# A hybrid decoder layer on one Trainium2 core: gate columns in column groups, the small delta-net inverse by blocks of four and doubling, product groups farther apart

## The chip, the core and the metric

The kernel runs on one NeuronCore of one Trainium2 chip. The metric is the device time of one execution in microseconds; three runs of the kernel before gave a median of 2695.42 us (2695.19 to 2695.53). Engine names are those of the profile: PE multiplies matrices (PEld loads its weights), DVE, ACT and POOL work elementwise, SP only issues DMAs.

## What is computed

One layer of a decoder on 512 new positions of one sequence and on 8 short sequences of 8 positions that carry states, 576 columns in all, everything in fp32. The part that matters here, cut from the reference:

```python
h = _rmsnorm(x, norm_mix_g)                       # x: 576 x 2048
proj = jnp.einsum('bld,de->ble', h, w_in)         # q, k, v, z of 8 delta-net heads, 4 mLSTM heads, and 24 gate columns
beta = jax.nn.sigmoid(dn_b)                       # gate columns: one row per head
g = -jnp.exp(dn_A_log) * jax.nn.softplus(dn_a + dn_dt_bias)
logf = jax.nn.log_sigmoid(ml_f + ml_f_bias)
...
G = jnp.cumsum(g, axis=-1)                        # delta net, by chunks
lower = jnp.where(strict, jnp.einsum('nbhik,nbhjk->nbhij', kb, k) * decay, 0.0)
a_mat = lower + jnp.eye(c)
u = solve(a_mat, v * beta[..., None])             # unit lower triangular
w = solve(a_mat, kb * jnp.exp(G)[..., None])
...
x = x + einsum(mix, w_out); x = x + ConvFFN(rmsnorm(x)); final rmsnorm
```

The triangular solves are done with the explicit inverse of each 128x128 unit triangle.

## The kernel before

Activations lie transposed: 16 tiles of 128 features by 576 columns (`KT` = 16, `NT` = 576, `HALF` = 288). A dense product of fp32 operands is made of three products of their high and low parts (line 198, `three`): per k-step of 128 features 2 halves x 3 products = 6 matmuls of 128x288, and a dense tile of 128 output features (`dense`) has 16 k-steps, 96 matmuls. Its weights come as two units of 128x1024 (512 KB), which `load_unit` brings (line 129, two raw buffers) and splits: ACT casts the high part (`wh`, line 120), DVE subtracts for the low part (`wl`, line 121), two buffers each.

PE's order is the order in which the program is written (`manual_schedule`); the other engines' order comes from a scheduler with priorities. Between the k-steps of the dense tiles a job list is ticked (`tick`, once a k-step): each job is a generator, and `yield n` means that its next piece is written n k-steps later. So the dense tiles fill PE, and the pieces of the heads are strewn between them; a piece whose operands are late stops PE, since nothing behind it overtakes.

- `startup` (line 332) loads `par` (all small parameters, POOL queue), the 16 tiles of x (line 351) and the first weight units, forms the scaled high and low parts `ah`, `al` (lines 356 and 357), and then squares x on ACT (line 363) and adds the squares on DVE and POOL in turn (lines 365 and 366).
- `gates` loads the constants `con` and the convolution state `dnst` on the POOL queue, makes small tables, and multiplies the padded tile of gate columns as the first dense tile of all, 96 matmuls into two PSUM banks.
- `gate_rows` waits 14 k-steps, sums the squares over the features with two fp32 matmuls of ones (line 256, 128x288 each), makes the reciprocal root `rstd`, and 6 k-steps later starts a chain of some 20 operations on rows of 576 columns: softplus, sigmoid, cumulated sums (lines 419 to 502). Transposes by PE (line 514) follow 30 + 30 k-steps later.
- The mixer multiplies q, k, v and z of head after head (4 dense tiles a head). `conv_in` takes a finished tile from PSUM with `rstd` (lines 536 to 538) and makes the causal convolution on DVE. As soon as the gate rows are done and the head before the last is finished, `dn_head` starts: groups of products with `yield 1` between (transposes of k at 608; k'k at 635; k'q at 646, whose PSUM DVE reads at 647; transposes of v at 657 and 662; DVE frees a bank at 628), then the inverse.
- `inverse` (line 779) first inverts the 16x16 diagonal blocks on DVE: POOL masks them, they go through DRAM (`ud`) into 40 lanes of 16x16, 14 steps of substitution of two operations each (lines 815 and 817) invert them, and they come back through DRAM (`xd`, `cx`); after `yield YJ + more` DVE spreads them (834), transposes (836), and PE doubles the blocks to 32, 64 and 128 (843 to 890). `more` is `YZ` = 5 for the first head.

After the 12 heads come the output projection, the convolutional FFN (line 1283 is its seven-product scheme) and the final norm, which the change does not touch.

Of the kernel before, what the change touches and what calls it, by code (L numbers as in the profile page):

```python
# [10 lines left out]
AF = mybir.ActivationFunctionType  # L11
ALU = mybir.AluOpType

P = 128
D = 2048
KT = 16
# [3 lines left out]
NT = SEQ + NB * LS  # L20
HALF = NT // 2
# [9 lines left out]
EPS = 1e-6  # L31
LV = (16, 32, 64)
SB = 16
# [5 lines left out]
YI = 8  # L39
YZ = 5  # L40
YS = 11
# [17 lines left out]
NIN = len(IN_ORDER)  # L59
NR = 23  # L60
NPL = 3
KB1 = 5
YP = 14
# [5 lines left out]
class Layer:  # L69
# [78 lines left out]
    def plain_weights(self):  # L148
        for name, n in (("w_in", NIN), ("w_out", KT), ("w_up", 2 * NPL - 2)):
            for t in range(n):  # L150
# [133 lines left out]
    def mixer(self):  # L284
# [47 lines left out]
    def startup(self):  # L332
        nc, I = self.nc, self.I
        self.par = self.cp.tile([P, NPAR], F32, tag="par", name="par")
        nc.gpsimd.dma_start(out=self.par, in_=I["par"])
        self.ones = self.cp.tile([P, P], F32, tag="ones", name="ones")
        nc.vector.memset(self.ones, 1.0)
        self.eps6 = self.cp.tile([P, 1], F32, tag="eps6", name="eps6")
        nc.vector.memset(self.eps6, EPS)
        self.epsh = self.cp.tile([P, 1], F32, tag="epsh", name="epsh")  # L340
        nc.vector.memset(self.epsh, EPS * EPS * P)
        self.rstd = self.cp.tile([P, NT], F32, tag="rstd", name="rstd")

        self.xh, self.xl = [], []
        acc = [self.r(), self.r()]
        xs = []
        acts = [self.new_act(k) for k in reversed(range(KT))][::-1]
        for k in range(KT):
            x = self.r()
            xs.append(x)  # L350
# [4 lines left out]
            g = self.par[:, G1 + k:G1 + k + 1]  # L355
            nc.scalar.activation(hi, x, AF.Copy, scale=g)
            nc.vector.scalar_tensor_tensor(out=lo, in0=x, scalar=g, in1=hi.bitcast(F32), op0=ALU.mult, op1=ALU.subtract)
            self.xh.append(hi)
            self.xl.append(lo)
        for k in range(KT):  # L360
            e = nc.gpsimd if k % 2 else nc.vector
            sq = acc[k] if k < 2 else self.r()
            nc.scalar.activation(sq, xs[k], AF.Square)
            if k > 1:
                e.tensor_tensor(out=acc[k % 2], in0=acc[k % 2], in1=sq, op=ALU.add)
        nc.vector.tensor_tensor(out=acc[0], in0=acc[0], in1=acc[1], op=ALU.add)
        self.acc = acc


    def gates(self):  # L370
        nc, I, O = self.nc, self.I, self.O
        V, A, Pl = nc.vector, nc.scalar, nc.gpsimd
        self.con = self.p1.tile([P, NCON], F32, tag="con", name="con")
        Pl.dma_start(out=self.con, in_=I["con"])
        self.ident = self.con[:, C_ID:C_ID + P]
        self.dnst = self.p1.tile([P, 24, 9, 3], F32, tag="dnst", name="dnst")
        Pl.dma_start(out=self.dnst, in_=I["dn_conv"])
        self.cwh = self.p1.tile([P, 96], F32, tag="cwh", name="cwh")
# [22 lines left out]

        outs = [self.psr()[:, 0:HALF] for _ in range(2)]
        self.dense(outs)
        return self.spawn(self.gate_rows(outs))

    def gate_rows(self, outs):
        nc, I, O = self.nc, self.I, self.O
        V, A, Pl = nc.vector, nc.scalar, nc.gpsimd
        yield 14
        self.rms_bc(self.acc[0], self.rstd)  # L410
        gr = self.r()
        for hf in range(2):
            sl = slice(hf * HALF, (hf + 1) * HALF)
            V.tensor_tensor(out=gr[:, sl], in0=outs[hf], in1=self.rstd[:, sl], op=ALU.mult)
        yield 6
        edge = self.tc.issue_after(self.last_evac.ins)
        edge.__enter__()
        y = self.r()
        V.tensor_scalar(out=y, in0=gr, scalar1=self.par[:, GB:GB + 1], scalar2=self.con[:, C_SG:C_SG + 1], op0=ALU.add, op1=ALU.mult)
        R1, R2, R3 = self.r(), self.r(), self.r()  # L420
        for t in (R1, R2, R3):
            Pl.memset(t, 0.0)
        th = self.r()
        A.activation(th[0:8], gr[0:8], AF.Tanh, scale=0.5)
        V.tensor_scalar(out=R1[0:8], in0=th[0:8], scalar1=0.5, scalar2=0.5, op0=ALU.mult, op1=ALU.add)

        e = self.r()
        A.activation(e, y, AF.Abs)
        A.activation(e, e, AF.Exp, scale=-1.0)
        d = self.r()  # L430
        V.tensor_scalar(out=d, in0=e, scalar1=2.0, scalar2=None, op0=ALU.add)
        V.reciprocal(d, d)
        V.tensor_tensor(out=e, in0=e, in1=d, op=ALU.mult)
        V.tensor_tensor(out=d, in0=e, in1=e, op=ALU.mult)
        p = self.r()
        V.tensor_scalar(out=p, in0=d, scalar1=1.0 / 17, scalar2=None, op0=ALU.mult)
        for c in (15, 13, 11, 9, 7, 5, 3):
            V.scalar_tensor_tensor(out=p, in0=p, scalar=1.0 / c, in1=d, op0=ALU.add, op1=ALU.mult)
        V.scalar_tensor_tensor(out=e, in0=p, scalar=1.0, in1=e, op0=ALU.add, op1=ALU.mult)
        sp = self.r()  # L440
        V.tensor_scalar(out=sp, in0=y, scalar1=0.0, scalar2=None, op0=ALU.max)
        V.scalar_tensor_tensor(out=sp, in0=e, scalar=2.0, in1=sp, op0=ALU.mult, op1=ALU.add)
        coef = self.sm(1, "coef", 1)
        A.activation(coef, self.par[:, AL:AL + 1], AF.Exp)
        V.tensor_scalar(out=coef, in0=coef, scalar1=-1.0, scalar2=None, op0=ALU.mult)
        V.tensor_scalar(out=sp, in0=sp, scalar1=coef, scalar2=None, op0=ALU.mult)
        edge.__exit__(None, None, None)
        yield 30
        edge = self.tc.issue_after(self.last_evac.ins)
# [54 lines left out]
        edge.__exit__(None, None, None)  # L504
        yield 30
        nc.sync.dma_start(out=self.rowd[0:8], in_=G[32:40])
# [78 lines left out]
    def dn_head(self, h, q, k, v, sz):  # L585
# [42 lines left out]
        V.tensor_tensor(out=KQ[0:64, sl4], in0=pk[0:64, P + 64:2 * P], in1=em[0:64, sl4], op=ALU.mult)  # L628
        yield 1

# [10 lines left out]
        next(inv)  # L641
        yield 1
        pr = self.psr()
# [4 lines left out]
        A.activation(q[:, 0:NT], q[:, 0:NT], AF.Square, scale=float(np.sqrt(EPS * P)))  # L648
        yield 1

# [49 lines left out]
        while not sample[3]:  # L700
            yield 1

# [75 lines left out]
    def inverse(self, U, res, more):  # L778
# [24 lines left out]
        nc.sync.dma_start(out=rows(ud), in_=cb)  # L803
        u, x = (lane[0:5 * nb, SB * SB * i:SB * SB * i + SB * SB].rearrange("p (r i) -> p r i", i=SB)
                for i in range(2))
        w = lane[0:5 * nb, 2 * SB * SB:2 * SB * SB + 4 * SB]
# [3 lines left out]
        V.memset(lane[0:5 * nb, SB * SB:2 * SB * SB:SB + 1], 1.0)  # L810
        self.tc.cur_priority -= PQ
        for j in range(SB - 2, 0, -1):
            n = SB - 1 - j
            wv = w[:, 0:j * n].rearrange("p (r i) -> p r i", r=j)
            V.tensor_tensor(out=wv, in0=u[:, 0:j, j:j + 1].to_broadcast([5 * nb, j, n]),
                            in1=x[:, j:j + 1, j + 1:].to_broadcast([5 * nb, j, n]), op=ALU.mult)
            V.tensor_tensor(out=x[:, 0:j, j + 1:], in0=x[:, 0:j, j + 1:], in1=wv, op=ALU.subtract)
        nc.sync.dma_start(out=lanes(xd), in_=x)
# [841 lines left out]
```

## Time and profile before

| | |
|---|---|
| three runs, median | 2695.42 us |
| profiled execution, its own time | 2699.44 us |
| its span, first to last instruction | 2697.7 us |
| PE busy | 2651.0 us, 19967 matmuls |
| DVE / ACT / POOL busy | 1994.0 / 1080.2 / 333.6 us |
| PE waits for other engines, the rows of the view summed | 34 us |

Numbers of the trace are of the one profiled execution; it lies 4.02 us (0.15%) above the median of the runs, 1.74 us of it outside of the span. Times of a row are from the span's start. In a timeline the columns are start, duration (of merged instructions together), engine, line, operation, tiles, count, and in brackets the idle time ahead and what ended it. In the view of the waits: engine, tile and line of the waiting instruction, who released it, then total, times, longest. In the view by windows each engine has its busy time and (x) the count of its instructions, PEclk is the granted TensorE clock. fp32 matmuls that are not in high and low parts appear as two records each.

### The profile page before, as it was taken

The numbers are of one execution on the slowest core, as the hardware profiler recorded it, in microseconds if no ns is written. First come the engines' busy times: TensorE is split into PE (matmuls) and PEld (weight loads), VectorE is DVE, ScalarE is ACT, GpSimd is POOL, SyncE is SP. The second block draws the span as 40 slices with busy tenths as digits, with TensorE's granted clock in tenths as the row PEclk, the third lists the DMA queues.
The fourth block names the chain that finished last, engine by engine and source line by source line (L and its number), as shares of the span: only waits on it lengthen the run. The fifth ranks groups of instructions, "written<-read, shape, count | busy, mean of one in ns | idle before, by whom it ended". The sixth has DMA issues, their size and how long they took to land.

```text
span 2697.7 us, 48872 instructions
## 1 busy us (share of the span) xinstructions
PE 2651.0 (98%) x19967; PEld 2607.0 (97%) x19967; DVE 1994.0 (74%) x3338; ACT 1080.2 (40%) x1704; POOL 333.6 (12%) x658
## 2 busy tenths in 40 slices
PE   7999999999999999998999999999999999999998
PEld 7998999999999999998999999999999999999998
DVE  7887777765544332389888888888888888888646
ACT  5334344443333322254444444444444433433324
POOL 3222322222211001101000000000000100000001
PEclk9999999999999999999999999999999999999999
DMA  5222222222333344444333333333333373342333
GB/s 195 85 77 87 90 91 91 91 88 92 114 113 104 115 135 135 135 123 150 107 111 108 108 108 108 108 108 108 108 108 109 109 256 94 106 146 71 122 97 100
DMA packets 112233, 304.02 MB, mean 113 GB/s; under 512 B 21912, under 2 KB 28184, under 8 KB 112008
## 3 DMA queue, kind: packets, MB, share of 16 engines
q1 hardware_dynamic: 107896, 291.17, 34.0%
q0 software_dynamic: 1872, 7.37, 0.8%
q8 instruction: 156, 2.56, 0.4%
q10 hardware_dynamic: 2240, 2.36, 0.3%
q14 instruction: 69, 0.57, 0.1%
HBM read 264.79 MB, written 36.06 MB: 112 GB/s over the span
## 4 chain that ended last, share of the span: by engine, by line
PE 89%; DVE 4%; DMA 1%; issue 0%; ACT 0%; POOL 0%; DVEq 0%; POOLq 0%; SPq 0%; ACTq 0%
PE pd L198 36%; PE pr L1283 31%; PE pd L1283 12%; PE pr L198 3%; PE pr L1509 1%; DVE bl L121 1%; DVE wl L121 1%; DMA r<-hid 0%; DVE r L1544 0%; PE pr L256 0%; PE pr L843 0%; PE pr L980 0%; PE pr L982 0%; PE pr L690 0%; PE pr L687 0%
## 5 line engine op out<-in xcount | busy, mean ns | idle before, releaser
L120 ACT CAST wh<-raw 128x1024 fp32r<-128x1024 f32 (+1 forms) x394 | 404.6, 1027 | 741.1 <-PE pd L198 400.2
L1283 PE MATMUL pr<-bh,wh 128*128 128x288 f32 x2120 | 626.8, 296 | 1.9 <-ACT bh L120 1.9
L1283 PE MATMUL pr<-bh,wl 128*128 128x288 f32 x2120 | 624.6, 295 | 0.5 <-DVE wl L121 0.5
L1283 PE MATMUL pr<-bl,wh 128*128 128x288 f32 x2120 | 624.3, 294 | 0.6 <-DVE bl L121 0.6
L121 DVE TENSOR_TENSOR wl<-raw,wh 128x1024 fp32r<-128x1024 f32 (+1 forms) x394 | 476.5, 1210 | 178.8 <-ACT wh L120 172.4
L198 PE MATMUL pd<-ah,wh 128*128 128x288 f32 x2496 | 560.3, 306 | 0.0
L198 PE MATMUL pd<-ah,wl 128*128 128x288 f32 x2496 | 534.5, 296 | 0.2 <-DVE wl L121 0.2
L198 PE MATMUL pd<-al,wh 128*128 128x288 f32 x2496 | 533.8, 296 | 0.0
L198 PEld LDWEIGHTS pd<-ah,wh 128*128 128x128 f32 x2496 | 401.0, 189 | 14.2 <-issue 7.7
L198 PEld LDWEIGHTS pd<-ah,wl 128*128 128x128 f32 x2496 | 401.8, 189 | 0.5 <-DVE wl L121 0.5
L198 PEld LDWEIGHTS pd<-al,wh 128*128 128x128 f32 x2496 | 401.7, 189 | 0.0
L1283 PEld LDWEIGHTS pr<-bl,wh 128*128 128x128 f32 x2120 | 400.0, 189 | 1.1 <-DVE bl L121 1.1
L1283 PEld LDWEIGHTS pr<-bh,wh 128*128 128x128 f32 x2120 | 398.4, 188 | 2.1 <-ACT bh L120 2.1
L1283 PEld LDWEIGHTS pr<-bh,wl 128*128 128x128 f32 x2120 | 398.9, 188 | 1.2 <-DVE wl L121 1.2
L120 ACT CAST wh<-s 128x1024 fp32r<-128x1024 f32 (+1 forms) x171 | 169.6, 992 | 361.2 <-DVE s L1248 142.2
L1283 PE MATMUL pd<-bh,wh 128*128 128x288 f32 x848 | 252.2, 297 | 5.6 <-ACT wh L120 5.6
L1283 PE MATMUL pd<-bh,wl 128*128 128x288 f32 x848 | 250.8, 296 | 1.7 <-DVE wl L121 1.7
L1283 PE MATMUL pd<-bl,wh 128*128 128x288 f32 x848 | 249.7, 294 | 0.0
L121 DVE TENSOR_TENSOR wl<-s,wh 128x1024 fp32r<-128x1024 f32 (+1 forms) x171 | 196.5, 1149 | 26.0 <-ACT wh L120 18.4
L1283 PEld LDWEIGHTS pd<-bh,wh 128*128 128x128 f32 x848 | 160.3, 189 | 6.1 <-ACT wh L120 6.1
L1283 PEld LDWEIGHTS pd<-bh,wl 128*128 128x128 f32 x848 | 160.6, 189 | 2.2 <-DVE wl L121 2.2
L1283 PEld LDWEIGHTS pd<-bl,wh 128*128 128x128 f32 x848 | 161.0, 190 | 0.0
(400 smaller groups left out, 3501.1 us busy)
## 6 DMA issues: line engine op xcount, KB each, us to landing
raw<-in_w_up SPq DMA_DIRECT2D x176, 512.0 KB
raw<-in_w_in SPq DMA_DIRECT2D x114, 512.0 KB
raw<-in_w_down SPq DMA_DIRECT2D x40, 512.0 KB
raw<-in_w_out SPq DMA_DIRECT2D x32, 512.0 KB
raw<-in_w_down SPq DMA_DIRECT2D x40, 384.0 KB
hid<-r SPq DMA_DIRECT2D x44, 288.0 KB
r<-hid SPq DMA_DIRECT2D x40, 288.0 KB
r<-in_xT SPq DMA_DIRECT2D x32, 288.0 KB
```

The lines of the kernel that those rows point to most:

```text
L120: nc.scalar.copy(hi, src)
L121: nc.vector.tensor_tensor(out=lo, in0=src, in1=hi.bitcast(F32), op=ALU.subtract)
L198: mm(outs[hf], w, x[:, hf * HALF:(hf + 1) * HALF], start=first and i == 0, stop=last and i == 2)
L1283: mm(out, w[:, ks], x[:, sl], start=k == 0 and i == 0, stop=k == nk - 1 and i == 2)
L1509: mm(pr[:, 0:n], w[:, ks], acts[kk][:, a * NT + sl.start:a * NT + sl.stop], start=kk == 0 and i == 0, stop=kk == FB - 1 and i == 2)
```

## The change

It does five things, all in the mixer.

1. The start: the weight unit of the first dense tile is loaded ahead of x, the next two behind the 8th and the 15th tile of x; the 16 columns of `par` that the scaling needs come alone on the POOL queue, and `par`, `con` and `dnst` go to the SP queue behind x. Fourteen fp32 matmuls of ones (`NW`) are put ahead of all others on PE.
2. The gate tile is no dense tile any more: the first dense tile is q of head 0, which ACT copies out of PSUM unscaled. The gate columns, 32 wide with POOL's scaling (`gate_weights`), are multiplied as plain fp32, x in four quarters of 144 columns, each quarter into its own 32 PSUM partitions (line 429; 64 matmuls). When PE has read a tile of x, DVE or ACT squares it in place (431, 433), and 64 matmuls with ones (438), in the same four column groups, sum the squares.
3. The chain of gate operations runs on 128x144 instead of 128x576. Two matmuls with ones (459) spread `rstd`, one small one (463) the per-row constants, two (503) bring the quarters back into rows.
4. In `inverse` the 14 steps become: two steps of substitution in the four 4x4 blocks at once, then doubling from 4 to 8 (two blocks) and from 8 to 16 (one), each by a product over a third axis (892) and a TENSOR_REDUCE over it (894), twice.
5. The product groups of a delta-net head stand 2 k-steps apart instead of 1, and `YZ` is 10.

```diff
-YZ = 5
+YZ = 10
+NW = 14
 ...
-            q, k, v = (self.conv_in(8 * i + h, self.dense()) for i in range(3))
+            if h == 0:
+                q0, pd = self.r(shape=[P, 2, HALF]), self.dense()
+                A.copy(q0, self.halves(pd))
+                pd = self.dense()
+                q, k = self.conv_in(0, q0), self.conv_in(8, pd)
 ...
-        nc.gpsimd.dma_start(out=self.par, in_=I["par"])
+        g1 = self.r(shape=[P, KT])
+        nc.gpsimd.dma_start(out=g1, in_=I["par"][:, G1:G1 + KT])
 ...
+        for _ in range(NW):
+            nc.tensor.matmul(pw[:, 0:P], self.ones, self.ones, start=True, stop=True)
 ...
+            if k in (0, 8, 15):
+                self.load_unit()
             nc.sync.dma_start(out=x, in_=I["xT"][k])
-            if k in (1, 3):
-                self.load_unit()
 ...
-            sq = acc[k] if k < 2 else self.r()
-            nc.scalar.activation(sq, xs[k], AF.Square)
-            if k > 1:
-                e.tensor_tensor(out=acc[k % 2], in0=acc[k % 2], in1=sq, op=ALU.add)
 ...
-        outs = [self.psr()[:, 0:HALF] for _ in range(2)]
-        self.dense(outs)
 ...
+        yield 20
+        for k in range(KT):
+            for s, t in quarters:
+                mm(pg[s], self.gw[:, k], self.xs[k][:, t], start=k == 0, stop=k == KT - 1)
+            if k % 2:
+                V.tensor_tensor(out=self.xs[k], in0=self.xs[k], in1=self.xs[k], op=ALU.mult)
+            else:
+                A.activation(self.xs[k], self.xs[k], AF.Square)
+        yield 5
+        ps = self.psr()[:, 0:Q]
+        for k in range(KT):
+            for s, t in quarters:
+                mm(ps[s], self.ones[:, 0:32], self.xs[k][:, t], start=k == 0, stop=k == KT - 1)
+        self.rsqrt_bc([(ps, slice(0, Q))], 1.0 / D, self.eps6, EPS, rq[:, 0], rq[:, 1], rq[:, 2])
 ...
+        yield 5
+        for sl in halves:
+            pr = self.psr()[:, 0:HALF]
+            mm(pr, self.ones, wide[:, sl], start=True, stop=True)
+            A.copy(self.rstd[:, sl], pr)
+        yield 4
 ...
-        yield 30
+        yield 28
+            mm(pr, there.rearrange("p g w -> p (g w)"), t5[:, sl], start=True, stop=True)
 ...
         next(inv)
-        yield 1
+        yield 2
 ...
-        for j in range(SB - 2, 0, -1):
-            n = SB - 1 - j
-            wv = w[:, 0:j * n].rearrange("p (r i) -> p r i", r=j)
-            V.tensor_tensor(out=wv, in0=u[:, 0:j, j:j + 1].to_broadcast([5 * nb, j, n]),
-                            in1=x[:, j:j + 1, j + 1:].to_broadcast([5 * nb, j, n]), op=ALU.mult)
-            V.tensor_tensor(out=x[:, 0:j, j + 1:], in0=x[:, 0:j, j + 1:], in1=wv, op=ALU.subtract)
+        for j in (2, 1):
+            V.tensor_tensor(out=wv, in0=U4[:, :, 0:j, j:j + 1].to_broadcast(full), in1=X4[:, :, j:j + 1, j + 1:].to_broadcast(full), op=ALU.mult)
+            V.tensor_tensor(out=X4[:, :, 0:j, j + 1:], in0=X4[:, :, 0:j, j + 1:], in1=wv, op=ALU.subtract)
+        for n in (4, 8):
+            for b in range(SB // (2 * n)):
+                for o, l, r in ((M, xb[:, 0:n, n:2 * n], xb[:, n:2 * n, n:2 * n]), (xb[:, 0:n, n:2 * n], xb[:, 0:n, 0:n], M)):
+                    V.tensor_tensor(out=tmp, in0=l.unsqueeze(2).to_broadcast(full),
+                                    in1=r.rearrange("p k i -> p i k").unsqueeze(1).to_broadcast(full), op=ALU.mult)
+                    V.tensor_reduce(out=o, in_=tmp, axis=mybir.AxisListType.X, op=ALU.add)
```

The instruction order moves at three places. First the start of SP's queue, on which the first matmul waits: `raw` is a weight unit, `r` a tile of x. Before:

```order
L351 DMA r_125<-in_xT 128x576
L351 DMA r_129<-in_xT 128x576
L129 DMA raw_131<-in_w_in 128x1024
L351 DMA r_139<-in_xT 128x576
L351 DMA r_143<-in_xT 128x576
L129 DMA raw_145<-in_w_in 128x1024
L351 DMA r_153<-in_xT 128x576
```

And now, from the 15th tile of x on; the first row of the queue is `L130 DMA raw_140<-in_w_in`, then eight tiles of x, a unit, and seven tiles:

```order
L364 DMA r_208<-in_xT 128x576
L130 DMA raw_212<-in_w_in 128x1024
L364 DMA r_218<-in_xT 128x576
L378 DMA r_222<-in_w_in 128x512
L373 DMA par<-in_par 128x515
L387 DMA con<-in_con 128x853
L378 DMA r_225<-in_w_in 128x512
L378 DMA r_228<-in_w_in 128x512
L378 DMA r_231<-in_w_in 128x512
L390 DMA dnst<-in_dn_conv 128x648
L130 DMA raw_318<-in_w_in 128x1024
L130 DMA raw_374<-in_w_in 128x1024
```

The first unit moved from the third place to the first, and the parameters, the gate weights (`in_w_in 128x512`) and the states now stand between the last tile of x and the fourth unit.

Second PE, in the second dense tile. Before, the last k-steps of q of head 0 (`pd_388`) with the two matmuls of ones:

```order
L198 MATMUL pd_388<-al_96,wh_336 128x288 x2
L198 MATMUL pd_388<-ah_95,wl_337 128x288 x2
L256 MATMUL pr_491<-r_91,ones 128x288
L256 MATMUL pr_493<-r_91,ones 128x288
L198 MATMUL pd_388<-ah_93,wh_336 128x288 x2
L198 MATMUL pd_388<-al_94,wh_336 128x288 x2
L198 MATMUL pd_388<-ah_93,wl_337 128x288 x2
L198 MATMUL pd_528<-ah_123,wh_391 128x288 x2
```

Now, in k of head 0 (`pd_373`), the end of the sums of squares by column groups and, five k-steps later (these rows are the fifth), the matmuls that spread `rstd` (`r_592`):

```order
L199 MATMUL pd_373<-ah_110,wh_320 128x288 x2
L199 MATMUL pd_373<-al_111,wh_320 128x288 x2
L199 MATMUL pd_373<-ah_110,wl_321 128x288 x2
L459 MATMUL pr_653<-r_592,ones 128x288
L459 MATMUL pr_656<-r_592,ones 128x288
L199 MATMUL pd_373<-ah_108,wh_320 128x288 x2
L199 MATMUL pd_373<-al_109,wh_320 128x288 x2
L199 MATMUL pd_373<-ah_108,wl_321 128x288 x2
```

The 96 matmuls of the gate tile that stood ahead of all this are gone; 16 x 4 matmuls `32x144` of line 429 stand behind the 5th k-step of `pd_373`, those of line 438 behind the 10th, and the pair with ones behind the 15th.

Third DVE, in the inverse of head 2 (`r_2710` before, `r_2957` and `r_2958` now, are its lanes; lines 536 to 551 and 594 to 609 are the convolution of another tile). Before, the last third of the 28 operations:

```order
L121 TENSOR_TENSOR wl_2840<-raw_2837,wh_2839 128x1024
L815 TENSOR_TENSOR r_2710<-r_2710 40x44
L538 TENSOR_TENSOR r_2939<-pd_2740,rstd 128x8x8
L817 TENSOR_TENSOR r_2710<-r_2710 40x4x11
L543 TENSOR_SCALAR r_2946<-r_2939,cwh 128x600
L815 TENSOR_TENSOR r_2710<-r_2710 40x36
L545 SCALAR_TENSOR_TENSOR r_2946<-r_2939,cwh,r_2946 128x600
L817 TENSOR_TENSOR r_2710<-r_2710 40x3x12
L545 SCALAR_TENSOR_TENSOR r_2946<-r_2939,cwh,r_2946 128x600
L815 TENSOR_TENSOR r_2710<-r_2710 40x26
L545 SCALAR_TENSOR_TENSOR r_2946<-r_2939,cwh,r_2946 128x600
L817 TENSOR_TENSOR r_2710<-r_2710 40x2x13
```

Now, the whole doubling:

```order
L892 TENSOR_TENSOR r_2957<-r_2958 40x64 x2
L894 TENSOR_REDUCE r_2957<-r_2957 40x16 x2
L892 TENSOR_TENSOR r_2957<-r_2958,r_2957 40x64 x2
L894 TENSOR_REDUCE r_2958<-r_2957 40x4x4 x2
L892 TENSOR_TENSOR r_2957<-r_2958 40x512
L894 TENSOR_REDUCE r_2957<-r_2957 40x64
L607 SCALAR_TENSOR_TENSOR r_3075<-r_3075,r_3082 128x512
L892 TENSOR_TENSOR r_2957<-r_2958,r_2957 40x512
L122 TENSOR_TENSOR wl_3094<-raw_3091,wh_3093 128x1024
L894 TENSOR_REDUCE r_2958<-r_2957 40x8x8
```

Where almost every operation of the inverse had one of another tile between it and the next, two stand within the doubling; the others stand ahead of it.

More of the change, by code (lines that the diff above doesn't have):

```diff
@@ L148, in plain_weights @@
     def plain_weights(self):
-        for name, n in (("w_in", NIN), ("w_out", KT), ("w_up", 2 * NPL - 2)):
-            for t in range(n):
+        for name, t0, n in (("w_in", 1, NIN), ("w_out", 0, KT), ("w_up", 0, 2 * NPL - 2)):
+            for t in range(t0, n):
                 for u in range(2):
@@ L290, in mixer @@
         for h in range(DNH):
-            q, k, v = (self.conv_in(8 * i + h, self.dense()) for i in range(3))
+            if h == 0:
[4 more added lines that the diff above has]
+            else:
+                q, k = (self.conv_in(8 * i + h, self.dense()) for i in range(2))
+            v = self.conv_in(16 + h, self.dense())
             pd = self.dense()
@@ L359, in startup, with gate_weights @@
             self.xl.append(lo)
-        for k in range(KT):
-            e = nc.gpsimd if k % 2 else nc.vector
-            sq = acc[k] if k < 2 else self.r()
-            nc.scalar.activation(sq, xs[k], AF.Square)
-            if k > 1:
-                e.tensor_tensor(out=acc[k % 2], in0=acc[k % 2], in1=sq, op=ALU.add)
-        nc.vector.tensor_tensor(out=acc[0], in0=acc[0], in1=acc[1], op=ALU.add)
-        self.acc = acc
+        for k in range(0, KT, 4):
+            self.gate_weights(k, g1)
+        nc.sync.dma_start(out=self.par, in_=I["par"])
+    def gate_weights(self, k, g1):
+        raw = self.r(shape=[P, 4, 4, 32])
+        self.nc.sync.dma_start(out=raw, in_=self.I["w_in"][0][k // 8][:, k % 8 * P:(k % 8 + 4) * P].rearrange("p (k g w) -> p k g w", k=4, g=4))
+        self.nc.gpsimd.tensor_tensor(out=self.gw[:, k:k + 4].rearrange("p k (g w) -> p k g w", g=4), in0=raw[:, :, :, 0:8],
+                                     in1=g1[:, k:k + 4].unsqueeze(2).unsqueeze(3).to_broadcast([P, 4, 4, 8]), op=ALU.mult)
     def gates(self):
@@ L373, in gates @@
         self.con = self.p1.tile([P, NCON], F32, tag="con", name="con")
-        Pl.dma_start(out=self.con, in_=I["con"])
+        nc.sync.dma_start(out=self.con, in_=I["con"])
         self.ident = self.con[:, C_ID:C_ID + P]
         self.dnst = self.p1.tile([P, 24, 9, 3], F32, tag="dnst", name="dnst")
-        Pl.dma_start(out=self.dnst, in_=I["dn_conv"])
+        nc.sync.dma_start(out=self.dnst, in_=I["dn_conv"])
         self.cwh = self.p1.tile([P, 96], F32, tag="cwh", name="cwh")
@@ L416, in gate_rows @@
         edge = self.tc.issue_after(self.last_evac.ins)
         edge.__enter__()
[L418 to L425, printed above, removed]
@@ L427, in gate_rows @@
-        e = self.r()
+        c = lambda i: cq[:, i:i + 1]
+        gr, t4, t5 = self.r(shape=[P, 3, Q]), self.r(shape=[P, 3, Q]), self.r()
+        gr, y, val = (gr[:, i] for i in range(3))
+        e, d, p = (t4[:, i] for i in range(3))
+        V.tensor_tensor(out=gr, in0=pg, in1=rq[:, 0], op=ALU.mult)
+        V.tensor_scalar(out=y, in0=gr, scalar1=c(0), scalar2=c(2), op0=ALU.add, op1=ALU.mult)
+        Pl.memset(t5, 0.0)
+        A.activation(val, gr, AF.Tanh, scale=0.5)
+        V.tensor_scalar(out=val, in0=val, scalar1=c(3), scalar2=c(3), op0=ALU.mult, op1=ALU.add)
@@ L803, in inverse @@
         nc.sync.dma_start(out=rows(ud), in_=cb)
-        u, x = (lane[0:5 * nb, SB * SB * i:SB * SB * i + SB * SB].rearrange("p (r i) -> p r i", i=SB)
-                for i in range(2))
-        w = lane[0:5 * nb, 2 * SB * SB:2 * SB * SB + 4 * SB]
+        L = 5 * nb
+        u, x = (lane[0:L, SB * SB * i:SB * SB * i + SB * SB].rearrange("p (r i) -> p r i", i=SB) for i in range(2))
         nc.sync.dma_start(out=u, in_=lanes(ud))
```

98 lines of the change are left out of this document (67 added, 31 removed).

## Prediction

> **What bounds the kernel now.** I read the page first, then the waits of PE, then the beginning by windows and by timeline.
>
> ```profile
> span 2697.7 us, 48872 instructions
> PE 2651.0 (98%) x19967; PEld 2607.0 (97%) x19967; DVE 1994.0 (74%) x3338; ACT 1080.2 (40%) x1704; POOL 333.6 (12%) x658
> PE 89%; DVE 4%; DMA 1%; issue 0%; ACT 0%; POOL 0%; DVEq 0%; POOLq 0%; SPq 0%; ACTq 0%
> ```
>
> PE is busy for 98% of the span and 89% of the chain that ended last. So a change can bring time in three ways only: fewer PE instructions, shorter ones, or shorter waits of PE. The waits (releaser, total, times, longest):
>
> ```profile
> PE pr L198 <- ACT wh L120: 10.4, 1, 10.4
> PE pd L1283 <- ACT wh L120: 5.6, 2, 4.0
> PE pr L256 <- DVE r L366: 4.3, 1, 4.3
> PE pr L843 <- DVE r L836: 3.1, 1, 3.1
> PE pr L657 <- DVE r L628: 1.9, 2, 1.5
> PE pr L771 <- DVE r L647: 1.0, 1, 1.0
> PE pr L646 <- ACT r L684: 0.6, 1, 0.6
> PE pr L662 <- DVE r L628: 0.6, 1, 0.6
> PE pr L687 <- ACT r L684: 0.5, 1, 0.5
> PE pr L866 <- DVE cb L799: 0.3, 1, 0.3
> ```
>
> Line 1283 belongs to the FFN, which stays. Lines 198 and 256 are the start (14.7 us); the other seven are the delta net, 8.0 us together. The beginning by windows (PE busy with its count, later the granted clock):
>
> ```profile
> 10.41:13.78 3.37, 3.37 (x12) 3.06 (x13) 2.86 (x4) 3.08 (x6) 0.36 (x3) 1.00 1.03 406
> 13.78:25.04 11.26, 11.26 (x85) 11.24 (x85) 10.91 (x15) 11.26 (x17) 0.00 (x0) 1.00 1.02 397
> 41.76:47.94 6.18, 6.18 (x22) 5.61 (x23) 2.28 (x4) 1.95 (x3) 0.00 (x0) 0.50 0.18 67
> ```
>
> At full pace a 128x288 matmul takes 11.26/85 = 0.1325 us: a k-step of six is 0.80 us, a dense tile of 96 is 12.7 us. In the first window it takes 3.37/12 = 0.28 us, though the clock column reads 1.00 there; in the third, behind the wait of 4.3 us, also 0.28, at a granted clock of 0.50. The last number is GB/s: loads run at about 400.
>
> **The start, old.** By 47.94 us PE has done the gate tile, q of head 0 but its last k-step (90 matmuls), and behind the two matmuls of ones (four records) 22 - 4 = 18 more: 108 matmuls that the new kernel needs too, 14.3 us at full pace. The other 47.94 - 14.3 = 33.6 us are start, gate tile, sums, wait and half clock.
>
> **The start, new.** Rows of the old start give the durations:
>
> ```profile
> 3.67 1.28 ACT L356 ACT_TABLE_LOAD   x1 [3.67 <-DMA r<-in_xT]
> 9.31 1.04 ACT L120 CAST wh<-raw 128x1024 fp32r<-128x1024 f32 x1 [2.52 <-DMA raw<-in_w_in]
> 10.39 1.25 DVE L121 TENSOR_TENSOR wl<-raw,wh 128x1024 fp32r<-128x1024 f32 x1 [2.68 <-ACT wh L120]
> 11.56 0.80 DVE L357 SCALAR_TENSOR_TENSOR al<-r,par,ah 128x576 fp32r<-128x576 f32 x1
> ```
>
> The first load (288 KB) landed at 3.67. The unit now ahead has 224 KB more, 0.57 us at 400 GB/s: 4.25; cast until 5.3, low part 6.55, `al` about 7.3. PE can begin with the products of the high parts, so I set its start at 7.0. Ahead of the tile's end SP must bring 16 x 288 + 3 x 512 = 6144 KB, 15.7 us at that rate from 2.9 on (3.67 less the first load's 0.74), so the last tile of x lands at 18.7; the third unit just before it costs ACT 1.04 and DVE 1.25, then `al` 0.80: about 21.0, and the tile ends near 21.6. Start and stalls together are 21.6 - 12.7 = 8.9 us. The 28 records of the 14 matmuls of ones run while PE would wait and price at nothing if they end by 7; they also keep PE from idling ahead of the tile. If they don't raise the clock the first 3.4 us run at 0.28 us again, +1.8.
>
> For the column groups the old trace has fours of 128x32 matmuls (16 records are four fours):
>
> ```profile
> 179.86 0.65 PE L747 MATMUL pr<-st,kqs 128*32 128x128 f32 x16
> 180.43 0.53 PE L198 MATMUL pd<-ah,wh 128*128 128x288 f32 x2
> 651.91 1.07 PE L1004 MATMUL pr<-st,qim 128*32 128x257 f32 x16
> 652.92 0.53 PE L198 MATMUL pd<-ah,wh 128*128 128x288 f32 x2
> 220.85 1.13 PE L256 MATMUL pr<-r,ones 128*128 128x288 f32 x4
> 221.91 0.41 PE L753 MATMUL pr<-r,pick 128*32 128x128 f32 x4
> ```
>
> From each start to the next row: 0.57 us at 128 columns, 1.01 at 257, so 0.44/(4 x 129) = 0.85 ns a column and 0.123 us for a four of 144. One group has 128 records, 32 fours: 3.9 us, with 0.13 fixed and about 0.2 for the change of shape (first dense row 0.53, not 0.42) 4.25; two groups 8.5. The last two rows: a fp32 record of 288 columns out of groups takes 1.06/4 = 0.265 us, half that at 144; so four that ran one after another would take 0.53. The trace says that four run side by side.
>
> The Trainium skill is more careful here: "TensorE: Matmul & The Clock Gate", section "Measured speedup vs the span model", gives 3.07 times for four row tiles and 2.38 for three column tiles. With 3.07 a group would be an estimated 17.0/3.07 = 5.5 us, and the whole forecast 2.5 us later. This trace's fours beat it (0.53/0.123).
>
> Lines 459 and 503, a pair like line 256's each: 1.06 us each; line 463: 0.3. New other work: 8.9 + 8.5 + 2.4 = 19.8 us. The start **saves 33.6 - 19.8 = 13.8 us.**
>
> That needs three covers.
>
> ```profile
> L363 ACT ACTIVATE r<-r 128x576 f32<-128x576 f32 x16 | 9.8, 673 | 0.0
> 34.05 1.28 ACT L244 ACT_TABLE_LOAD   x1
> 43.12 0.50 ACT L244 ACTIVATE rstd<-pr,eps 128x288 f32<-128x288 f32 x1 [7.79 <-PE pr L256]
> 62.01 3.75 DVE L432 RECIPROCAL r<-r 128x576 f32<-128x576 f32 x1
> 85.35 1.35 DVE L456 TENSOR_TENSOR_SCAN r<-r,r 128x576 f32<-128x576 f32 x1
> ```
>
> Eight squares on ACT (0.67, 5.4 us) and eight on DVE run while PE is in the gate group and five k-steps (4.25 + 4.0): hidden, with 2 us to spare. Then table load 1.28, root and four small DVE operations, about 3.2 us, against five k-steps, 4.0. The old gate chain took 85.35 - 62.01 = 23.3 us from reciprocal to scan, with convolutions between; at a quarter of the width these two rows alone fall by some 3.8 us, to 19.5, and further rows stand ahead of it; PE comes to line 503 28 k-steps (22.4 us) behind line 463. That cover is thin, 0 to 2 us. If it goes, PE stands there, as at 41.76.
>
> **The delta net.** Its work by groups and rows:
>
> ```profile
> L815 DVE TENSOR_TENSOR r<-r 40x14 f32<-40x14 f32 (+6 forms) x112 | 25.1, 224 | 2.2
> L817 DVE TENSOR_TENSOR r<-r 40x14 f32<-40x14 f32 (+6 forms) x112 | 21.3, 190 | 2.4
> 242.86 0.67 DVE L647 TENSOR_TENSOR r<-pr,r 128x512 f32<-128x512 f32 x1
> 469.88 0.69 DVE L836 STREAM_TRANSPOSE r<-r 128x512 f32<-128x512 f32 x1
> 471.51 1.05 PE L843 MATMUL pr<-r,r 128*128 128x128 f32 x8
> 271.21 1.05 PE L843 MATMUL pr<-r,r 128*128 128x128 f32 x7 [3.11 <-DVE r L836]
> ```
>
> Old: 28 operations a head, (25.1 + 21.3)/8 = 5.8 us alone, nearly each with one of another tile behind it. New: 16 operations. Four of substitution at 0.19 make 0.8; four products and four TENSOR_REDUCEs of 64 elements, between that and the 512 row, I estimate at 0.25, 2.0; two products and two reduces of 512 at 0.68, like L647, 2.7. Together 5.5 us: alone it saves nothing, but there are only half as many places for a convolution to slip between. A TENSOR_REDUCE stands nowhere in the trace; the lower bound is the 0.19 of the small rows, the upper one is the reciprocal's pace, 3752/576 = 6.5 ns an element, 3.3 us for 512.
>
> The wider gaps move pieces later in PE's row, which costs PE nothing, since dense tiles fill the row in either case. Each product group gets a k-step, 0.80 us, more. L771's 1.0 falls to 0.2, L657's two waits (1.5 and 0.4) to 0.7, the other four small ones to nothing, and L843's 3.1 with two k-steps and a shorter chain to nothing. 0.9 of 8.0 remains; I allow 1.4 for waits that appear anew where the order has changed (the units and columns of heads 0 to 2): **it saves 5.7 us**, between 0 and 8.
>
> **Sum.** -13.8 - 5.7 = -19.5 us against the profiled execution's own 2699.44, which is 2679.9. It lies 4.02 us above the median of the runs; by the median 2695.42 - 19.5 = 2676.
>
> **Rivals.**
> A. Delta-net waits only move: what L843 loses another tile of DVE's row gains, since DVE's work there is the same. 13.8 us are saved, 2681.6. For it: 74% of DVE busy and 5.5 us against 5.8. Against it: most waits are under a k-step long.
> B. The new consumers come too early: line 503 (or 459, or the gate weights, which are loaded last) stands 4 us, and PE then goes to half clock as it did at 41.76, which costs 3 us more: 2695.42 - 19.5 + 7 = 2683.
> C. TENSOR_REDUCE at the reciprocal's pace: 6.7 for the two large ones, 1.7 for four small (64 x 6.5 ns), with 3.1 of the others 11.5 us, 5.7 longer than the old. At 469.88 line 836 ended 0.94 us ahead of line 843; two k-steps make 2.5; 3.2 us late in each of six heads (not 0 and 2, which stand later) are 19.2 and leave the time as it was, 2695. The point at which PE begins to wait is a chain of 8.3 us. The Trainium skill calls tensor_reduce the slowest operation of DVE and advises to restructure ("VectorE: DVE Perf Modes", "Rules for kernel authors"), but still at one element a cycle; no run here shows one yet.
> D. The column groups don't run side by side: the 144-column fours go one after another at 0.53 us, 17.0 us a group, 12.7 more than forecast, 25.4 in both. 2676 + 25.4 = 2701, slower. It decides from 0.43 us a four (0.123 + 19.5/64). L747 and L1004 speak against it; for it only that these four write one bank and read four different column ranges.
>
> **How the numbers follow.** Forecast 0.60, A 0.17, B 0.13, C 0.06, D 0.04. A measurement of this kernel can tell about 0.2%, 5.4 us. Forecast, A and B lie below 2690.0: faster 0.90; C within: 0.06; D above 2700.8: 0.04. The range takes in A and B, upwards with the clock's 1.8 or the skill's 2.5 on top, to 2687; downwards a start without stalls (1.9), no new waits (1.4) and a little more, to 2671.
>
> **What would show it.** Right: first dense row near 7 us, first tile ended near 21.6, at 0.13 us a matmul throughout; from line 429's first row to the next dense row 4.25 us, the same for 438; no wait at lines 459 and 503 over 1 us; no clock of 0.50 ahead of the FFN; TENSOR_REDUCE of 512 elements near 0.7 us; the old L843's wait gone and no other delta-net wait over 1 us. Wrong: a group of 17 us (D), a reduce of 3 us (C), an idle PE of 4 us with half clock behind it (B), delta-net waits that again sum to 8 us (A).

## The result, and the profile after

The changed kernel takes 2710.27 us (median of 5, 2709.35 to 2712.78) against 2695.53 us before (5 runs, 2695.19 to 2697.49): the ratio is 1.0055, 95% interval 1.004 to 1.0069. It is slower by 14.7 us where 2676 us and a gain were forecast. The profiled execution took 2710.27 us, with a span of 2708.5; the spans differ by 10.8 us.

The page of the changed kernel, the same three lines as before:

```profile
span 2708.5 us, 49206 instructions
PE 2657.2 (98%) x20161; PEld 2612.9 (96%) x20161; DVE 1990.6 (73%) x3244; ACT 1074.5 (40%) x1702; POOL 324.8 (12%) x672
PE 81%; DVE 8%; issue 2%; DMA 1%; ACT 1%; POOL 1%; SPq 0%; DVEq 0%; ACTq 0%; POOLq 0%
```

PE's share of the chain fell from 89% to 81%, DVE's doubled from 4% to 8%: PE now stands more often for DVE. PE's waits (line numbers moved: 715, 720, 829, 920 and 943 are the old 657, 662, 771, 843 and 866):

```profile
PE pr L920 <- POOL r L626: 3.2, 1, 3.2
PE pr L720 <- ACT r L754: 2.5, 2, 1.9
PE pr L829 <- DVE r L705: 2.5, 1, 2.5
PE pd L199 <- DVE al L368: 2.4, 3, 0.9
PE pr L943 <- DVE Xs L911: 2.3, 1, 2.3
PE pr L943 <- DVE r L934: 2.1, 3, 0.9
PE pr L720 <- DVE r L686: 2.0, 1, 2.0
PE pr L720 <- DVE r L705: 1.9, 1, 1.9
...
PE pr L741 <- DVE rr L736: 1.3, 1, 1.3
PE pr L734 <- DVE S L751: 1.3, 1, 1.3
PE pr L715 <- ACT r L670: 1.3, 1, 1.3
```

The waits of 10.4 and 4.3 us of the start are gone, as forecast, and the 3.1 us of the old line 843 have become 3.2, now put down to POOL; but new waits stand at nearly every other kind of piece of the delta net, most of them between 1 and 2.5 us. The start by timeline:

```profile
1.06 5.46 PE L355 MATMUL pr<-ones 128*128 128x128 f32 x28 [1.06 <-DVE epsh L350]
6.43 0.53 PE L199 MATMUL pd<-ah,wh 128*128 128x288 f32 x2
27.00 4.13 PE L429 MATMUL pr<-r,r 128*32 128x144 f32 x128
31.06 0.53 PE L199 MATMUL pd<-ah,wh 128*128 128x288 f32 x2
35.24 4.13 PE L438 MATMUL pr<-r,ones 128*32 128x144 f32 x128
43.39 1.13 PE L459 MATMUL pr<-r,ones 128*128 128x288 f32 x4
```

The first dense row stands at 6.43 us (forecast 7.0), a column group takes 31.06 - 27.00 = 4.06 us (4.25), and lines 459 and 503 don't wait. The first dense tile ended at 23.1 us, not near 21.6. To say where the rest went I take the same dense matmul in both traces: the first of the 7th dense tile of the heads starts at 112.08 us before and at 98.05 now (14.0 earlier; 13.8 were forecast), the first of the 37th at 631.09 and 642.32. (Over all profiles below, the 7th tile starts between 111.0 and 112.9 us with the old start and between 97.9 and 99.5 with the new one, so the gain is known to about 1 us.) Between these two starts (length, PE busy with its count, later the granted clock), first before, then now:

```profile
112.08:631.09 519.01, 510.59 (x3998) 486.98 (x3997) 376.56 (x924) 212.24 (x497) 148.87 (x194) 1.00 0.28 88
```

```profile
98.05:642.32 544.27, 519.23 (x4007) 495.39 (x4006) 392.03 (x837) 212.08 (x501) 150.98 (x198) 0.98 0.27 85
```

The stretch is 25.3 us longer. PE is idle for 544.27 - 519.23 = 25.0 us in it, 16.6 more than before (8.4), and busy for 8.6 us more with nearly the same matmuls (4007 records against 3998): the clock is at half for 17 us in this stretch, and before not at all. Nearly all of the loss is waits of the delta net and the half clock behind them.

### The profile page after: what moved, and what is told of

Read it like the earlier page. It is cut to its first block, busy times and chain, and to the rows that moved or that the text cites. A ratio compares the mean times of both kernels' runs of the same rounds, so it can differ in the third digit from the quotient of the medians.

```text
span 2708.5 us, 49206 instructions
## 1 busy us (share of the span) xinstructions
PE 2657.2 (98%) x20161; PEld 2612.9 (96%) x20161; DVE 1990.6 (73%) x3244; ACT 1074.5 (40%) x1702; POOL 324.8 (12%) x672
## 4 chain that ended last, share of the span: by engine, by line
PE 81%; DVE 8%; issue 2%; DMA 1%; ACT 1%; POOL 1%; SPq 0%; DVEq 0%; ACTq 0%; POOLq 0%
PE pr L1360 31%; PE pd L199 29%; PE pd L1360 12%; PE pr L199 3%; PE pr L1586 1%; DVE r L603 1%; DVE wl L122 1%; DMA r<-hid 1%; DVE bl L122 0%; DVE r L892 0%; DVE r L1621 0%; PE pr L1057 0%; PE pr L1059 0%; DVE r L894 0%; ACT wh L121 0%
```

## The experiments

Four theories were set against each other. **T1**: the doubling holds DVE in one block. **T2**: the wider gaps cost. **T3**: the earlier start costs, since every head then stands elsewhere against the weight units. What grew out of the first runs is **P**: DVE takes its row in a fixed order, the window between a piece of PE and the piece that needs DVE's answer is about as long as DVE's row in it, and any of the three parts puts other work of DVE into some window.

All results; "stretch" is the one from the 7th to the 37th dense tile, "idle" PE's idle time in it, "over" PE's busy time above the kernel before's 510.6 us. Kernels of a group ran on the same chip with runs of the kernel before beside them. The last three columns are of the one profiled execution of each kernel, which lies between 2.9 us below the median of its runs (inverse alone) and 4.6 us above it (gaps, compensated); they say where the time stands, the ratio says what a kernel costs.

| kernel | us | before there | ratio, 95% interval | stretch | idle | over |
|---|---|---|---|---|---|---|
| before | 2695.5 | | | 519.0 | 8.4 | 0 |
| changed | 2710.3 | 2695.5 | 1.0055 (1.0040 to 1.0069) | 544.3 | 25.0 | 8.6 |
| inverse alone | 2712.3 | 2699.1 | 1.0047 (1.0033 to 1.0062) | 531.1 | 16.7 | 3.8 |
| gaps alone | 2725.7 | 2699.1 | 1.0096 (1.0081 to 1.0111) | 543.2 | 26.3 | 6.4 |
| start alone | 2701.3 | 2699.1 | 1.0010 (1.0001 to 1.0020) | 535.3 | 19.6 | 5.1 |
| start + inverse | 2717.3 | 2699.1 | 1.0064 (1.0048 to 1.0081) | 553.3 | 27.7 | 15.0 |
| start, gate wait 13 | 2685.0 | 2698.4 | 0.9949 (0.9932 to 0.9965) | 517.8 | 7.0 | 0.2 |
| gaps, compensated | 2704.0 | 2698.4 | 1.0020 (1.0011 to 1.0029) | 526.2 | 13.7 | 2.0 |
| inverse, no priority | 2697.5 | 2698.4 | 0.9995 (0.9986 to 1.0005) | 517.6 | 6.5 | 0.6 |
| start 13 + inverse, no priority | 2684.4 | 2698.4 | 0.9947 (0.9932 to 0.9962) | 517.4 | 6.5 | 0.3 |
| changed, gate wait 13 | 2705.0 | 2697.6 | 1.0025 (1.0015 to 1.0036) | 538.9 | 21.6 | 6.8 |
| the same, no priority | 2711.5 | 2697.6 | 1.0047 (1.0034 to 1.0061) | 544.4 | 23.9 | 10.0 |
| all parts, shifts undone | 2692.6 | 2697.6 | 0.9977 (0.9968 to 0.9986) | 525.1 | 12.1 | 2.4 |
| gaps from head 3 on | 2685.3 | 2698.6 | 0.9951 (0.9937 to 0.9964) | 516.8 | 5.5 | 0.7 |

**Each part alone.** The new inverse in the kernel before:

```diff
-        for j in range(SB - 2, 0, -1):
...
+        for j in (2, 1):
...
+        for n in (4, 8):
```

> The kernel before with the new inverse alone. Three theories of where the changed kernel lost some 24 us between the fifth and the 34th dense tile: (T1) the doubling holds DVE in one block and makes the next head late; (T2) the wider gaps between product groups; (T3) the earlier start, which moves every head against the weight units. T1: near 2719 us (2695.5 + 24). T2 and T3: 2690 to 2697, as before or a little less.

Slower by 13.2 us (2712.33 against 2699.13): neither as before, as T2 and T3 had it, nor T1's 24. The gaps in the kernel before:

```diff
-YZ = 5
+YZ = 10
...
-        yield 1
+        yield 2
```

> The kernel before with product groups 2 k-steps apart and YZ = 10, nothing else. T2: near 2719 us. T1 and T3: 2690 to 2697 us, and the wait of 3.1 us of head 2's line 843 gone or less.

Slower by 26.6 us, even more than T2 asked for. In its trace PE waits 8.4 and 4.8 us for the first doubling products of heads 2 and 0, and 8.8 us together at the third kind (line 866) in heads 4 to 6. (This edit, like the change itself, also doubles the step of a waiting loop at a head's end. The loop moved nothing: wherever the later pieces were put back, as in "gaps, compensated", the norms of all heads stand at the same k-steps as before, 198, 230, 299 and so on.) The start and gates alone (against the changed kernel):

```diff
-YZ = 10
+YZ = 5
...
-        yield 2
+        yield 1
...
-        for n in (4, 8):
...
+        for j in range(SB - 2, 0, -1):
```

> The new start and gates alone, with the old inverse and the old gaps. The start saves 13.9 us by the position of the dense tiles. T1 and T2: near 2682 us, delta-net waits of PE some 8 us in all. T3: 2703 to 2710 us, delta-net waits of 20 us and more.

2.2 us slower: the 14.1 us that the start saves in this trace (112.08 against 97.94) are lost again, most of them in one wait (11.0 us). Start and inverse together:

```diff
-YZ = 10
+YZ = 5
...
-        yield 2
+        yield 1
```

> The new start with the new inverse, old gaps (groups 1 apart, YZ = 5). T1: near 2706 us or more (2682 + 24). T2: near 2682 us. T3: 2703 to 2710 us. If only inverse and gaps together cost the 24 us: 2682.

Slower by 18.2 us. So T1, T2 and T3 each hold for their own part and none alone: every part brings waits, at different places. In the inverse's run the one that repeats is in three heads (waits of PE):

```profile
PE pr L683 <- DVE rr L678: 9.0, 3, 3.0
```

DVE and PE around one of the three, by timeline:

```profile
384.95 0.38 PE L676 MATMUL pr<-S,r 128*128 128x128 f32 x2
390.71 0.46 PE L683 MATMUL pr<-rr,r 128*128 128x128 f32 x2 [3.00 <-DVE rr L678]
```

```profile
386.95 0.43 DVE L834 TENSOR_TENSOR r<-r 40x64 f32<-40x64 f32 x2
...
388.18 1.20 DVE L121 TENSOR_TENSOR wl<-raw,wh 128x1024 fp32r<-128x1024 f32 x1
389.31 0.99 DVE L834 TENSOR_TENSOR r<-r 40x512 f32<-40x512 f32 x1
390.24 0.33 DVE L678 SCALAR_TENSOR_TENSOR rr<-pr,cols,r 128x128 f32<-128x128 f32 x1
```

Line 676 was done at 385.3; `rr` (line 678), of the head whose state runs on meanwhile, is taken up at 390.24, behind the next head's products and reduces, which the priority `PQ` draws ahead. In the start's run the wait of 11 us is head 2's first doubling product; DVE's and SP's rows of its inverse:

```profile
258.42 0.28 DVE L867 TENSOR_SCALAR r<-r 40x256 f32<-40x256 f32 x1
275.22 0.17 DVE L875 TENSOR_TENSOR r<-r 40x14 f32<-40x14 f32 x1
279.57 0.69 DVE L892 TENSOR_TENSOR r<-cx,con 128x512 f32<-128x512 f32 x1 [4.18 <-DMA cx<-xd]
```

```profile
275.42 0.30 SPq L876 DMA_DIRECT2D xd<-r  x1
277.60 0.38 SPq L879 DMA_DIRECT2D cx<-xd  x1
```

The 28 operations take 17.0 us from 258.42 to 275.39, where they are 5.8 us of work: the convolutions, the weight splits and the output norm of head 1 stand between them. Then the way through DRAM takes 4.2 us, and PE, which came at 270.1, goes on at 281.11.

**The start put back in phase.** By PE's row in k-steps of the dense tiles, heads 0 and 2 began at 101 and 207 in the kernel before and at 114 and 220 in the start's run; heads 1 and 3 to 7 stood alike in both. One number undoes that:

```diff
-        yield 26
+        yield 13
```

> The new start and gates alone, with the last wait of the gate job 13 k-steps instead of 26, so that heads 0 and 2 begin at the same k-steps of the dense tiles as in the kernel before (101 and 207, not 114 and 220). Theory P (what costs is where the pieces of neighbouring heads meet in DVE's row, and the start only moved heads 0 and 2 to a bad place): the wait of 11 us of head 2's first doubling product falls to about 3 as in the kernel before, and the time is 13 to 16 us below that of the new start with 26, near 2699 - 14 = 2685. Rival R (the new start costs by itself, through its loads on SP's queue and the smaller lead of the gate rows): as with 26, 2699 to 2703, or worse, with new waits at the transposes of the gate rows.

2685.04 us: P's number, and head 2's wait is 1.45 us instead of 11.04 (DVE's first and last row of its inverse, and PE's first doubling product):

```profile
237.55 0.28 DVE L867 TENSOR_SCALAR r<-r 40x256 f32<-40x256 f32 x1
251.23 0.17 DVE L875 TENSOR_TENSOR r<-r 40x14 f32<-40x14 f32 x1
256.61 1.16 PE L901 MATMUL pr<-r,r 128*128 128x128 f32 x8 [1.45 <-DVE r L894]
```

The same 28 operations now take 251.40 - 237.55 = 13.9 us, 3.1 less. That is a third of the 9.6 us: counted from the head's first transpose on PE, the row also begins 3.5 us sooner (18.1 us behind it, not 21.6), the way behind the row is 0.5 shorter, and PE itself comes 2.4 us later to the product. Nothing of the start was taken back; only the place of two heads was. R falls.

**The inverse without priority.**

```diff
-PQ = 1000
+PQ = 0
```

> The kernel before with the new inverse, its small blocks without the raised priority (PQ = 0 instead of 1000). In DVE's row of heads 4 to 6 the operation that makes rr then stands ahead of the products and reduces of 64 elements, not behind the product of 512. Theory T1 in the form that the first runs left (the doubling is a block that rr waits for, 3.0 us of PE in three heads, with half clock behind them): these waits are gone, 2699 to 2703. Rival (the time of the reduces themselves): stays near 2712.

2697.53 us, 1.5 us below the range that was expected, and PE no longer waits for `rr`, which now stands ahead of the 64-element products:

```profile
386.01 0.34 DVE L678 SCALAR_TENSOR_TENSOR rr<-pr,cols,r 128x128 f32<-128x128 f32 x1
386.27 0.43 DVE L834 TENSOR_TENSOR r<-r 40x64 f32<-40x64 f32 x2
```

So the new inverse as such costs nothing that can be measured, and saves nothing: 0.9995 with 1 inside the interval. (The old inverse without priority was not run, so what the priority alone is worth there isn't known.) Start and inverse with both numbers:

```diff
-PQ = 1000
+PQ = 0
...
-        yield 26
+        yield 13
```

> New start with the gate job's wait of 13, new inverse without raised priority, old gaps. If the costs of the start's shift and of the inverse's place are both undone: 2685 to 2690. If either is not: 2697 or more.

2684.39 us, 0.6 below the range for both costs undone; it is the fastest of all, by 14.0 us against the kernel before (0.9947, 0.9932 to 0.9962). It can't be told from the start alone at 13 (2685.04).

**The gaps.** Wider gaps, but with the later pieces at their old place:

```diff
-        yield 1
+        yield 2
...
-        yield YI
+        yield YI - 3
```

> The kernel before with product groups 2 k-steps apart, but the wait behind the last group 3 k-steps shorter (5 instead of 8) and YZ = 5, so that the doubling products and all that follows stand at the k-steps of before. Theory P: 2695 to 2702, the waits of 3 us at the fifth product of the doubling in heads 3 and later gone. Rival: wider gaps cost by themselves (a head's row of PSUM banks and buffers is held longer): 2715 to 2726.

2703.97 us, between the two ranges, 2.0 above P's: of 26.6 us 5.6 are left. Heads 3 to 7 wait no more than 0.4 us anywhere; what is left stands in heads 0 to 2, 10.4 us of it in head 2's first doubling product. Then the changed kernel with the gate wait of 13 alone, and that without priority:

```diff
-        yield 26
+        yield 13
```

> The changed kernel with the gate job's last wait 13 instead of 26, so that head 0 begins where it began before; wider gaps, YZ = 10 and the doubling at raised priority stay. Theory P says that the gaps and the priority each bring their own collisions: waits of 15 us and more remain, 2695 to 2710. Rival (the start's shift of heads 0 to 2 was all): 2680 to 2686.

```diff
-PQ = 1000
+PQ = 0
...
-        yield 26
+        yield 13
```

> As the run before, and the doubling without raised priority. Theory P: what is left is the gaps with YZ = 10, which alone cost 26 us at the old inverse, of which the wait of line 843 in head 2 (8.4) and its half clock should go with the shorter chain: 2690 to 2705.

2705.0 and 2711.5 us: the shift of the start was not all, and the second came out above its range. Without priority the third kind of doubling product (line 943) waits 2.3 us in three heads, with it 0.6. Now all parts with all shifts undone; against the kernel just named only two numbers differ:

```diff
-YZ = 10
+YZ = 5
...
-        yield YI
+        yield YI - 3
```

> All parts of the change with their shifts undone: gate job's wait 13, no raised priority, groups 2 k-steps apart but 5 k-steps behind the last one, YZ = 5. Theory P: as the new start with the inverse without priority (2684), less the 3 to 4 us of small waits at the product groups that the wider gaps take away: 2679 to 2683. Rival (wider gaps cost by themselves, the 5.6 us of the run with gaps and shorter wait): 2687 to 2692.

2692.57 us: 18.9 us less by three k-steps in every head and five more in head 0, with the gaps as wide. (Head 2 starts when head 0 is done, so its first doubling product moves by eleven, from k-step 250 to 239.) The time is 0.6 us above the rival's range and far from P's: head 2's first doubling product still waits 8.3 us. This kernel and the one just named show the mechanism best. In the slower of the two, in head 4, PE's second kind of doubling product (line 932) stands at 402.55, and the third kind (line 943) waits:

```profile
402.55 1.05 PE L932 MATMUL pr<-r,r 128*128 128x128 f32 x8
409.10 1.12 PE L943 MATMUL pr<-r,r 128*64 128x64 f32 x8 [2.31 <-DVE r L934]
```

The answer comes behind 2.6 us of other work, of which the weight split alone takes 1.88. DVE's row there, where lines 594 to 596 take a finished tile from PSUM, 122 splits weights, and 933 and 934 answer line 932:

```profile
404.72 0.45 DVE L594 TENSOR_TENSOR r<-pd,rstd 128x288 f32<-128x288 f32 x1
...
405.51 1.88 DVE L122 TENSOR_TENSOR wl<-raw,wh 128x1024 fp32r<-128x1024 f32 x1
407.31 0.67 DVE L933 TENSOR_TENSOR r<-r,pr 128x512 f32<-128x512 f32 x1
408.35 0.70 DVE L934 STREAM_TRANSPOSE r<-r 128x512 f32<-128x512 f32 x1
```

With the doubling three k-steps earlier the answer stands ahead of the finished tile, and PE doesn't wait:

```profile
402.63 0.68 DVE L933 TENSOR_TENSOR r<-r,pr 128x512 f32<-128x512 f32 x1
403.34 0.71 DVE L934 STREAM_TRANSPOSE r<-r 128x512 f32<-128x512 f32 x1
403.98 0.42 DVE L594 TENSOR_TENSOR r<-pd,rstd 128x288 f32<-128x288 f32 x1
```

Last, the gaps only where they brought no wait, against the start and inverse with both numbers:

```diff
-        yield 1
+        yield 2 if h > 2 else 1
...
-        yield YI
+        yield YI - 3 if h > 2 else YI
```

> New start with the gate job's wait 13, new inverse without raised priority, and the wider gaps (2 k-steps, then 5) only for heads 3 to 7; heads 0 to 2 keep the old gaps. Theory P: the wait of 8.3 us of head 2's first doubling product, which the version with gaps in every head had, is gone with its half clock, and heads 3 to 7 lose their small waits (0.4 and 1.0 us): 2681 to 2685. Rival (the gaps cost in the later heads too): 2688 or more.

2685.33 us, 0.3 above P's range: head 2's first doubling product no longer waits, and the gaps cost nothing in heads 3 to 7. They bring nothing that can be measured either (2684.39 without them, on another chip). So the wait of 8.3 us came from the wider gaps of heads 0 to 2; which of the three heads' gaps make it was not separated. DVE's row of head 2's inverse, its first operation and the finished tile behind it (line 594), with the gaps in every head:

```profile
240.63 0.52 DVE L866 TENSOR_SCALAR r<-r 40x256 f32<-40x256 f32 x1 [1.20 <-DMA r<-ud]
242.25 0.44 DVE L594 TENSOR_TENSOR r<-pd,rstd 128x288 f32<-128x288 f32 x1
```

And with the old gaps in heads 0 to 2:

```profile
238.54 0.28 DVE L866 TENSOR_SCALAR r<-r 40x256 f32<-40x256 f32 x1
244.53 0.44 DVE L594 TENSOR_TENSOR r<-pd,rstd 128x288 f32<-128x288 f32 x1
```

In the first the tile comes when one operation of the substitution is done, in the second when only the last reduce is left. From its first operation to its last the inverse takes 15.3 us in the first and 9.2 in the second, and it begins 21.3 us behind the head's first transpose against 18.3.

## Why the prediction was wrong

**The start** was right as a step: 13.8 us forecast, 14.0 measured by position, and 13.3 us as a whole kernel (2685.04 against 2698.37) once the heads stand where they stood. Most of its terms held: column groups 4.06 us each against 4.25, no wait at lines 459 and 503. The squares and the root stayed covered. One term was short: start and stalls were set at 21.6 - 12.7 = 8.9 us and took 23.1 - 12.7 = 10.4, of which 2.4 are waits for the low parts (line 368's row; 1.9 were set for all stalls). It was made up elsewhere: the two groups took 0.4 us less, lines 459, 463 and 503 took 1.7 us instead of 2.4, and the transposes of the gate rows, which the sum left out, 0.9 less than before. So that the sum agrees to 0.2 us is in part luck. Rivals B and D, which were about this part, fell.

**The delta net** is the step that failed, and two sentences hold the fault. "The wider gaps move pieces later in PE's row, which costs PE nothing, since dense tiles fill the row in either case" looks at PE's row alone: the pieces' answers come from DVE, and DVE's row has its own fixed places (a finished tile every 16 k-steps, a weight split every 8, the norm of the head before). A piece that moves by 3 k-steps changes sides with one of them, and DVE's work slips ahead of its answer: 2.6 us in the two kernels compared at lines 932 and 943. And "it saves 5.7 us, between 0 and 8": nothing in the trace excluded a loss, and I gave the term none. It measured 25.3 us the other way. Of the 25.3 us 16.6 are waits, net of those that went, where 1.4 were allowed "for waits that appear anew".

**The shift of the heads** was no term at all, although the order showed it: the heads 0 and 2 now stand 13 and 21 k-steps later against the dense tiles (head 2 at 228, not 207), and head 4 two later. The 13 alone took back 16.3 us (the stretch of the start alone, 535.3 against 519.0), more than the start's gain of 14.1 in that run.

**The inverse**: its size was nearly right (a TENSOR_REDUCE of 512 elements 0.67 us, forecast 0.68; of 64, 0.2 against 0.25), the products of 512 were not (1.05 us, not 0.68), so that the whole takes some 5.9 us a head against 5.5 forecast and 5.8 before:

```profile
133.64 1.05 DVE L892 TENSOR_TENSOR r<-r 40x512 f32<-40x512 f32 x1
135.27 0.68 DVE L894 TENSOR_REDUCE r<-r 40x64 f32<-40x512 f32 x1
```

So C fell: the reduce is no slower here than the product. I wrote that there are "only half as many places for a convolution to slip between" and gave that no price. Its price is `rr`: 9.0 us of waits at the raised priority, none without.

**Rival A** came nearest (the waits move, since DVE's work stays the same), but as a ceiling of harm it was wrong: it let the sum of waits stand at 8 us. The sum is not conserved; before, the phases were such that it was small. **The half clock** was priced only at the start (rival B). It made 8.6 of the 25.3 us.

What stays open: why the parts don't add (start alone +2.2 us, inverse alone +13.2, both +18.2; start, inverse and gaps only +14.7). Each combination puts the rows of DVE into a new order, and the table only says where each stands; a rule that gives the waits of a combination from those of its parts was not found. Nor were the two numbers of the gaps, 2 k-steps and `YZ` = 10, run one by one. Whether a longer wait ahead of head 2's doubling would carry the gaps there too was not tried.

## What to carry to other kernels

Where one engine's order is written out by hand and the others follow in fixed order, a piece's place is worth as much as its cost: before moving it, list what the answering engine does between question and answer, and compare that sum with the window. Price a shift of the whole work against a periodic load (here the finished tiles and weight splits) like an edit of its own, and undo it first when a change that saves work comes out slower; here one number, 26 to 13, turned +2.2 into -13.3 us.

## What the runs showed of the hardware

Half clock came without an idle window. In the changed kernel PE's two waits that end at 145 and 147 us are short, and the window of the clock that begins at 145.37 us holds only the second, 1.98 us:

```profile
145.22 0.63 PE L715 MATMUL pr<-con,r 128*128 128x128 f32 x4 [1.29 <-ACT r L670]
147.83 0.27 PE L720 MATMUL pr<-con,r 128*64 128x128 f32 x1 [1.98 <-DVE r L686]
```

```profile
148.78:152.19 3.41, 3.41 (x16) 3.41 (x16) 3.34 (x7) 0.16 (x1) 0.98 (x3) 0.50 0.05 8
```

The granted clock changes only at multiples of 3.41 us. I counted PE's idle time (gaps above 0.3 us) in each such window at full clock, from PE's first instruction to its last, in the 14 profiles of this study. With 1.70 us or less no window was followed by half clock, with 1.80 us or more every one was, and between them (1.72 to 1.77) both happened. So about half a window of idle time is enough, and whether a wait of 2 to 3 us costs its clock depends on where the window's border cuts it: the wait of 3.11 us at 268 us of the kernel before had 1.7 us in one window, the rest in the next, and cost none. The Trainium skill ("TensorE: Matmul & The Clock Gate", section "What's actually happening") gives the same window and puts the half rate behind one idle window; here 1.98 us of idle time in one window did it.

Four column groups ran wholly side by side: 128 records of 144 columns in 4.06 us, where one after another, at half of the 0.265 us that a record of 288 columns takes, they would have taken an estimated 17.0.
